# A state-space branch with chunks of eight tokens for four, unpadded matrices and lags through DRAM

## The chip, the cores and the metric

The kernel runs on one core of a Trainium2 chip. The metric is the device time of one execution in microseconds (us), the median of repeated runs.

## What is computed

One layer of a hybrid backbone over 512 latent tokens of 1024 channels with a context of 256 tokens. A conditioning vector gives shifts and scales for a first RMS norm; one input projection gives queries, keys, values, the state-space input u and two gates. A bidirectional diagonal state-space model of 32 groups with 64 complex states and 16 channels each runs over context and latent tokens, next to grouped attention; both are gated and merged, and a gated MLP with a width-3 convolution follows.

```python
def scan(bu_re, bu_im):                      # per direction, over tokens
    s_re, s_im = lax.associative_scan(_ssm_combine, (a_re, a_im, bu_re, bu_im), reverse=reverse, axis=1)
...
bu = einsum('blgp,gnp->blgn', u, bbar)       # complex, bbar from lambda, dt and b by zero-order hold
y += einsum('blgn,gpn->blgp', s_re, c_re) - einsum('blgn,gpn->blgp', s_im, c_im)
y += u * d
```

## The kernel before, in words

All matrices are fp32 split into a rounded part and a remainder: `weight` (line 126 on) loads a 256 KB piece on SP's queue into one of three `wr` buffers, ScalarE rounds it to `wh` (L128) and an engine named by the caller subtracts to `wl` (L129). `mm3` then issues three TensorE instructions per product, all recorded at L120.

The planner below the kernel orders the instructions of each engine by their order in the text and by a simulated readiness, so work of later lines fills gaps of earlier ones; each engine and SP's queue then run in that fixed order. The projection `proj` of the gates, 16 times, the keys, the values and two queries have no link to the branch and interleave with it. The attention phase reuses the memory of the branch's pool, and the GELU of the branch's result `y` precedes attention's exponentials on ScalarE, because the activation tables are changed in a fixed order (`table`, `act`).

Front: squares and their sums give the reciprocal root (`rstd_first`); x and ctx are multiplied by it on VectorE; then for each of eight row blocks the modulation row comes from TensorE (`mod_sums`, `mod_turn`), ScalarE applies scale and shift twice (once rounded, once not), VectorE subtracts, and TensorE accumulates u in `ul` and `uc`.

The branch cuts time into chunks of four tokens, so a scan has 192 steps. Channels are handled in four blocks `s` of 128, each of four pairs `k` of groups. `u` is written to DRAM and read back once, as 32 rows per token of a chunk. Lines before `s5_in` turn the parameters into powers of the step; most of that is on POOL (`DE`). `s5_in` and `s5_out` multiply b and c by the powers on POOL and place the results by half-height VectorE additions (L319) into zero-padded matrices `wpad` and `hpad`; the matrix of lags inside a chunk comes from TensorE (`kps`), is transposed on VectorE and copied by 32 partitions into `tp`. `turn` makes the sine and cosine tables of a pair, the additions on POOL.

`s5_pair`, 16 times: four transposes (`gps`), a copy (`gt`), four drive products of 192 columns into `gp` (a two-bank tile, tag "s", two buffers), rotation by the tables on VectorE (`p`), six scans, the rotation back (`ts`, on POOL but for a few), and five readout products of 128 columns into `yps`. `s5_end` copies 32 partitions at a time to `y`.

The helper `tt` (L319) records all element-wise products and sums of the branch, whichever the engine.

## Time and profile before

| | us |
|---|---|
| median of 3 runs | 1072.75 (1072.25 to 1072.86) |
| profiled execution | 1073.12 |
| its span | 1071.3 |

| engine | busy us | share of the span |
|---|---|---|
| TensorE | 947.3 | 88% |
| VectorE | 585.3 | 55% |
| ScalarE | 451.4 | 42% |
| POOL | 510.7 | 48% |

The shares are means over stages with different limits. The stages are: parameters, first norm and u up to about 88 us; the branch beside the projections up to about 350; attention up to about 675; then the output projection and the MLP. A product in fp32 is two TensorE instructions, one of a rounded operand is one.

### The profile page before, as it was taken

Reading aid. Unit: us, or ns where it says so; the run is one execution under the profiler, and the core shown is the slowest. Engines: PE = TensorE matmul, PEld = TensorE weight load, DVE = VectorE, ACT = ScalarE, POOL = GpSimd, SP = SyncE. Lnnn points to the kernel's source line nnn. Section 1 sums busy time; section 2 is a strip of 40 time slices with the busy share of each in tenths; the row PEclk is TensorE's granted clock in tenths of the full one; section 3 lists DMA queues with packets and bytes.
Section 4 is the critical chain, followed back from the end, with each engine's and each line's share of the span. In section 5 each row is a group of like instructions: output and inputs, shape, how many; then the busy total and the mean of one; then the engine's idle time right before and its main releaser. Section 6 shows DMA issues by size and latency. Waiting matters only on the chain.

```text
span 1071.3 us, 13697 instructions
## 1 busy us (share of the span) xinstructions
PE 947.3 (88%) x4978; PEld 770.2 (72%) x4978; DVE 585.3 (55%) x1069; ACT 451.4 (42%) x810; POOL 510.7 (48%) x496
## 2 busy tenths in 40 slices
PE   2978778898785898988989998999999999999996
PEld 1667677676674676756757688988888888888886
DVE  7544999979797766556655454543333323311103
ACT  6455345353532544343444234354444434433322
POOL 5865864536454335234220354055655556545553
PEclk9889989899898899998989999999999999999998
DMA  9515102121210131323223345023322332233332
GB/s 367 188 43 174 31 25 84 45 76 58 59 59 21 41 117 61 112 104 136 100 99 118 99 152 183 1 79 99 92 91 94 99 98 90 88 104 93 95 107 85
DMA packets 47604, 103.51 MB, mean 97 GB/s; under 512 B 5425, under 2 KB 11825, under 8 KB 43825
## 3 DMA queue, kind: packets, MB, share of 16 engines
q1 hardware_dynamic: 47536, 102.64, 29.1%
q8 instruction: 39, 0.64, 0.3%
q14 instruction: 29, 0.23, 0.1%
HBM read 98.95 MB, written 3.67 MB: 96 GB/s over the span
## 4 chain that ended last, share of the span: by engine, by line
PE 52%; DVE 13%; issue 8%; POOL 4%; ACT 3%; DMA 3%; DVEq 0%; POOLq 0%; ACTq 0%
PE up L120 23%; PE down L120 11%; PE proj L120 5%; PE po L120 3%; DVE p L319 2%; PE gb L120 2%; PE sc L120 2%; PE ga L120 2%; DMA wr<-wo 2%; DVE w L319 2%; POOL wl L129 1%; DVE nt L679 1%; DVE st L520 1%; ACT y L542 1%; DVE wl L129 1%
## 5 line engine op out<-in xcount | busy, mean ns | idle before, releaser
L129 POOL TENSOR_TENSOR wl<-wr,wh 128x512 fp32r<-128x512 f32 x194 | 253.3, 1324 | 369.3 <-ACT wh L128 362.1
L120 PE MATMUL up<-t,wh 128*128 128x512 f32 (+1 forms) x768 | 225.7, 378 | 1.6 <-DVE t L807 0.9
L128 ACT CAST wh<-wr 128x512 fp32r<-128x512 f32 x226 | 128.5, 609 | 110.6 <-PE down L120 36.1
L120 PEld LDWEIGHTS up<-t,wh 128*128 128x128 f32 x768 | 140.1, 188 | 32.1 <-DVE t L807 2.4
L120 PE MATMUL up<-t,wl 128*128 128x512 f32 (+1 forms) x384 | 144.8, 377 | 0.0
L120 PE MATMUL proj<-h,wh 128*128 128x512 f32 x384 | 129.7, 411 | 0.4 <-ACT wh L128 0.4
L120 PEld LDWEIGHTS proj<-h,wh 128*128 128x128 f32 x384 | 75.4, 197 | 19.0 <-DVE nb L718 1.5
L120 PE MATMUL proj<-h,wl 128*128 128x512 f32 x192 | 79.4, 413 | 4.9 <-DVE wl L129 4.9
L120 PEld LDWEIGHTS up<-t,wl 128*128 128x128 f32 x384 | 72.3, 188 | 14.6
L841 DVE SCALAR_TENSOR_TENSOR zc<-up,pv,zc 128x511 f32<-128x511 f32 x44 | 33.0, 751 | 88.4 <-ACT zc L840 88.4
L840 ACT ACTIVATE zc<-up,pv 128x512 f32<-128x512 f32 x44 | 34.1, 776 | 75.0 <-PE up L120 75.0
L319 DVE TENSOR_TENSOR w<-pw,pw 64x128 f32<-64x128 f32 x128 | 51.1, 431 | 22.9 <-POOL pw L319 20.6
L319 POOL TENSOR_TENSOR ts<-st,tab 128x512 f32<-128x512 f32 x28 | 39.4, 1424 | 34.0 <-DVE st L525 29.1
L872 DVE SCALAR_TENSOR_TENSOR x<-down,mods,x 128x512 f32<-128x512 f32 (+1 forms) x9 | 6.2, 691 | 87.8 <-PE down L120 87.8
L107 ACT ACTIVATE P<-sc,nb,rq 128x768 f32<-128x768 f32 x32 | 31.7, 993 | 52.3 <-DVE nb L718 32.5
L120 PEld LDWEIGHTS proj<-h,wl 128*128 128x128 f32 x192 | 38.1, 198 | 13.2 <-DVE wl L129 5.9
L717 DVE TENSOR_REDUCE nb<-sc 128x1 f32<-128x768 f32 x32 | 30.0, 952 | 31.0 <-PE sc L120 30.8
L120 PE MATMUL sc<-g,qh 128*128 128x512 f32 (+1 forms) x128 | 38.0, 363 | 7.4 <-ACT qh L128 5.5
L128 ACT CAST pth<-tps 128x512 fp32r<-128x512 f32 x48 | 27.9, 587 | 37.1 <-PE tps L730 31.2
L319 POOL TENSOR_TENSOR pw<-cb,hs 128x256 f32<-128x256 f32 x32 | 23.4, 747 | 38.4 <-DVE w L319 23.1
L120 PE MATMUL po<-ptl,g 128*128 128x512 f32 x48 | 23.6, 491 | 19.8 <-DVE ptl L129 19.7
L120 PE MATMUL yps<-ts,w 128*128 128x128 f32 x128 | 22.4, 312 | 20.1 <-DVE ts L319 11.5
(291 smaller groups left out, 2158.3 us busy)
## 6 DMA issues: line engine op xcount, KB each, us to landing
wr<-wup SPq DMA_DIRECT2D x88, 256.0 KB, 2.8
wmb<-wmB SPq DMA_DIRECT2D x16, 1024.0 KB, 5.8
wr<-wdn SPq DMA_DIRECT2D x40, 256.0 KB, 2.7
x<-x SPq DMA_DIRECT2D x4, 1024.0 KB, 6.5
g<-wmA SPq DMA_DIRECT2D x4, 1024.0 KB, 9.4
w<-wmA SPq DMA_DIRECT2D x4, 1024.0 KB, 11.2
wr<-wgs SPq DMA_DIRECT2D x16, 256.0 KB, 2.8
wr<-wga SPq DMA_DIRECT2D x16, 256.0 KB, 2.9
```

The lines of the kernel that those rows point to most:

```text
L107: i = A.activation(*a, **k).ins
L120: last[0] = T.matmul(ps, l, r, start=start, stop=stop).ins
L128: A.copy(hi, src)
L129: eng.tensor_tensor(lo, src, f(hi), op=OP.subtract)
L319: eng.tensor_tensor(o, a, b, op=op)
L520: V.tensor_tensor_scan(sv[0][:, ri, 0:192], rho[:, c0:c0 + 1].to_broadcast([128, 192]), p1[:, 0, ri], 0.0, op0=OP.mult, op1=OP.add)
L542: A.copy(y[32 * s:32 * s + 32, :, t::4], yps[32 * t:32 * t + 32].rearrange("p (k c) -> p k c", k=4))
L679: V.scalar_tensor_tensor(t, t, -0.5, xv, op0=OP.mult, op1=OP.mult)
L717: V.tensor_reduce(nb[:, b:b + 1], sv, axis=AX.X, op=OP.max)
L840: A.activation(z, ps, AF.Identity, scale=cw[1], bias=pv[:, PV_CB + i:PV_CB + i + 1])
L841: V.scalar_tensor_tensor(z[:, 1:512], ps[:, 0:511], cw[0], z[:, 1:512], op0=OP.mult, op1=OP.add)
L872: V.scalar_tensor_tensor(x1[i][:, c], ps[:, c], g2[:, i:i + 1], x1[i][:, c], op0=OP.mult, op1=OP.add)
```

## The change

Chunks have eight tokens, so a scan has 96 steps, and `u` has 16 rows per token. Two pairs of both directions go together: `s5_half` runs eight times, with eight scans of 96 columns each. Its operations are all on VectorE, those of `turn` too. `s5_build` makes the matrices `W` and `H` of a block without padding by six VectorE operations of 1024 elements each; a small `wpad` is filled by ScalarE. The lag matrix goes to DRAM and comes back shifted in eight pieces; `u` is read back per block, in eight pieces; the readout goes to DRAM and comes back as `y` in eight pieces. TensorE works in half arrays: drive products have 64 columns of weights, readout products 64 rows, and `y2` holds a two-bank tile of tag "s" for a whole block. The parameters' powers are computed on VectorE ahead of the first norm, for all exponents at once, with a change of activation tables there and back. The norm's multiply takes the modulation scale as well, which removes one ScalarE pass per row block. The gates' weight remainders go from VectorE to POOL. Host-side layouts of ctx, the parameters and `wglu` follow; the multiply after the GLU reads and writes tokens in the new order.

```diff
+TC = 8
+NC = (L + LC) // TC
+NL = L // TC
...
+    act(rho, ldt, AF.Exp, scale=float(TC))
...
+    def cmul(o, a, b, n):
+        c1, c2 = tz([8, 32], "bb", 2)[:, 0:n], tz([8, 32], "bb", 2)[:, 0:n]
+        br, bi = (b[:, None, i].to_broadcast([128, n, 32]) for i in range(2))
+        tt(c1, a[:, :, 0], br, OP.mult)
+        tt(c2, a[:, :, 1], bi, OP.mult)
+        tt(o[:, :, 0], c1, c2, OP.subtract)
+        tt(c1, a[:, :, 0], bi, OP.mult)
+        tt(c2, a[:, :, 1], br, OP.mult)
+        tt(o[:, :, 1], c1, c2, OP.add)
+    cmul(pw[:, 1:2], pw[:, 0:1], pw[:, 0], 1)
+    cmul(pw[:, 2:4], pw[:, 0:2], pw[:, 1], 2)
+    cmul(pw[:, 4:8], pw[:, 0:4], pw[:, 3], 4)
...
+    cmul(pf[:, 1:8], pw[:, 0:7], pf[:, 0], 7)
+    ws, hs = tz([2, 32, 8], "ws"), tz([2, 32, 8], "hs")
+    for o, i, up in ((ws, pf, 0), (hs, pw, 0)):
+        iv = i.rearrange("p e r (c d) -> p d r c e", d=2)
+        ov = o.rearrange("p r (c d) e -> p d r c e", d=2)
+        A.copy(ov[:, 0], iv[:, 0])
+        A.copy(ov[:, 1], iv[:, 1, :, :, ::-1])
...
-            V.tensor_tensor(src, src, rs, op=OP.mult)
-            A.activation(hi, src, AF.Identity, scale=am[:, k, m:m + 1], bias=shm[:, k, m:m + 1])
-            A.activation(src, src, AF.Identity, scale=am[:, k, m:m + 1], bias=shm[:, k, m:m + 1])
-            V.tensor_tensor(lo, src, f(hi), op=OP.subtract)
+            V.scalar_tensor_tensor(src, src, am[:, k, m:m + 1], rs, op0=OP.mult, op1=OP.mult)
+            A.activation(hi, src, AF.Identity, bias=shm[:, k, m:m + 1])
+            V.scalar_tensor_tensor(lo, src, shm[:, k, m:m + 1], f(hi), op0=OP.add, op1=OP.subtract)
...
+        us = k8("g12", [TC, NC + NL])
+        lat = ul[s // 2][:, s % 2].rearrange("p (c t) -> p t c", t=TC)[:, ::-1]
+        A.copy(us[:, :, NL:NC], uc[s // 2][:, 256 * (s % 2):256 * (s % 2) + 256].rearrange("p (t c) -> p t c", t=TC))
+        A.copy(us[:, :, 0:NL], lat)
+        V.tensor_copy(us[:, :, NC:NC + NL], lat)
+        ud = dram.tile([128, TC, NC + NL], F32, tag="ud", name="ud", bufs=4)
...
+    def s5_u(s):
+        u = tz([8, NC + NL], "u", 2)
+        for t in range(TC):
+            S.dma_start(u[16 * t:16 * t + 16], us_[s][:, t].rearrange("(j q) c -> q j c", j=8))
+        return u
...
+    def built(o, src, scal, s):
+        def by(a):
+            return scal[:, a, 8 * s:8 * s + 8, :, None].to_broadcast([128, 8, 8, 16])
+        b = [src[:, a, :, None, :].to_broadcast([128, 8, 8, 16]) for a in range(2)]
+        ov = [o[:, a].rearrange("p k (r q) -> p k r q", r=8) for a in range(2)]
+        for a in range(2):
+            t = tz([8, 8, 16], "t", 2)
+            tt(ov[a], b[0], by(a), OP.mult)
+            tt(t, b[1], by(1 - a), OP.mult)
+            tt(ov[a], ov[a], t, OP.add if a else OP.subtract)
+    def s5_build(s):
+        bb, cb_ = tz([2, 8, 16], "bb", 2), tz([2, 8, 16], "bb", 2)
+        S.dma_start(bb, io["sb"][s])
+        S.dma_start(cb_, io["sc"][s])
+        W, H = k8("k12", [2, 8, 128]), k8("w8", [2, 8, 128])
+        built(W, bb, ws, s)
...
+                src = ap_of(W[pa, ri, 0, 0:], [[256, 4], [128 + 112, 2], [1, 16]])
+                dst = ap_of(wpad[pa, ri, 0, g, 0:], [[64, 4], [32, 2], [1, 16]])
+                A.activation(dst, src, AF.Copy, scale=-1.0 if ri else 1.0)
+        built(H, cb_, hs, s)
...
+        for o, n, terms in ((0, 112, [(H[:, ri], 16, ri, 1) for ri in range(2)]),
+                            (112, 16, [(cb_[:, ri], 0, ri, d) for d in range(2) for ri in range(2)]),
+                            (128, 112, [(H[:, ri], 0, ri, 0) for ri in range(2)])):
+            for i, (m, c, ri, d) in enumerate(terms):
                 for k in range(4):
+                    T.matmul(kps[32 * k:32 * k + 32, o:o + n], wpad[:, ri, 2 * k + d].rearrange("p g q -> p (g q)"),
+                             m[:, 2 * k + d, c:c + n], start=i == 0, stop=i == len(terms) - 1, tile_position=(0, 32 * k))
+        lg = tz([240], "lg")
+        A.copy(lg, kps[:, 0:240])
+        V.scalar_tensor_tensor(lg[:, 112:128], cst[:, CS_D:CS_D + 16], sd[:, s:s + 1], lg[:, 112:128], op0=OP.mult, op1=OP.add)
+        ldr = dram.tile([128, 240], F32, tag="ldr", name="ldr", bufs=4)
+        S.dma_start(ldr, lg)
+        tp = tz([8, 128], "tp")
+        for r in range(TC):
+            S.dma_start(tp[16 * r:16 * r + 16], ldr[:, 16 * r:16 * r + 128].rearrange("(j q) l -> q j l", j=8))
+        blocks[s] = W, H, tp, s5_u(s)
...
+        wv, wq = tz([4, 6, 16], "t", 2), tz([4 * NC], "t", 2)
+        tt(wv, wa[:, c, :, None].to_broadcast([128, 4, 6, 16]), wb[:, c, None, :].to_broadcast([128, 4, 6, 16]), OP.add)
+        wv = wv.rearrange("p c a b -> p (c a b)")
         A.activation(wq, wv, AF.Identity, bias=magic)
         V.scalar_tensor_tensor(wv, wq, MAGIC, wv, op0=OP.subtract, op1=OP.subtract)
         A.activation(wq, wv, AF.Abs)
+        tab = tz([2, 4 * NC], "tab", 2)
+        act(tab[:, 0], wq, AF.Sin, scale=-TWO_PI_LO, bias=half_pi)
+        act(tab[:, 1], wv, AF.Sin, scale=-TWO_PI_LO)
+        tabs[n] = tab
...
+    def s5_drive(s, h):
+        W, H, tp, u = blocks[s]
+        gp = bank2("gp")
+        for k2 in range(2):
+            k = 2 * h + k2
+            gps = bank("gps", "b")
+            for d in range(2):
+                for ri in range(2):
+                    i = 2 * d + ri
+                    T.transpose(gps[:, 128 * i:128 * i + 128], W[:, ri, 2 * k + d], ident)
+            gt = tz([4, 128], "gt", 2)
+            A.copy(gt, gps.rearrange("p (i n) -> p i n", i=4))
+            for d in range(2):
+                c = slice(0, NC) if d else slice(NL, NL + NC)
+                o = NC * (2 * k2 + d)
+                for ri in range(2):
+                    for g in range(2):
+                        T.matmul(gp[64 * g:64 * g + 64, ri, o:o + NC], gt[:, 2 * d + ri, 64 * g:64 * g + 64],
+                                 u[:, 2 * k + g, c], start=True, stop=True, tile_position=(0, 64 * g))
+        return gp[:, :, 0:4 * NC]
+    def s5_half(s, h, gv, y2):
+        W, H, tp, u = blocks[s]
+        tab = tabs.pop(2 * s + h)
+        p1, p2, z = (tz([2, 4 * NC], "p", 3) for _ in range(3))
+        tt(p1, gv, tab[:, None, 0].to_broadcast([128, 2, 4 * NC]), OP.mult)
+        tt(p2, gv, tab[:, None, 1].to_broadcast([128, 2, 4 * NC]), OP.mult)
+        tt(p1[:, 0], p1[:, 0], p2[:, 1], OP.add)
+        tt(p1[:, 1], p2[:, 0], p1[:, 1], OP.subtract)
+        for i in range(4):
+            c = 8 * s + 4 * h + i
+            o = slice(NC * i, NC * i + NC)
             for ri in range(2):
+                zi, pi = z[:, ri, o], p1[:, ri, o]
+                if i % 2:
+                    zi, pi = zi[:, ::-1], pi[:, ::-1]
+                V.tensor_tensor_scan(zi, rho[:, c:c + 1].to_broadcast([128, NC]), pi, 0.0, op0=OP.mult, op1=OP.add)
+        q1, q2 = (t2().rearrange("p (r k c) -> p r k c", r=2, k=4) for _ in range(2))
+        zv = z.rearrange("p r (k d c) -> p d r k c", d=2, c=NC)
+        tv = tab.rearrange("p r (k d c) -> p d r k c", d=2, c=NC)
+        for j, q in enumerate((q1, q2)):
+            qv = q.rearrange("p r (k d) c -> p d r k c", d=2)
+            for d in range(2):
+                c = slice(1, 1 + NL) if d else slice(NC - NL - 1, NC - 1)
+                tt(qv[:, d], zv[:, d, :, :, c], tv[:, d, j, None, :, c].to_broadcast([128, 2, 2, NL]), OP.mult)
+        tt(q1[:, 0], q1[:, 0], q2[:, 1], OP.add)
+        tt(q1[:, 1], q1[:, 1], q2[:, 0], OP.subtract)
+        for k2 in range(2):
+            k = 2 * h + k2
+            o = slice(NL * k, NL * k + NL)
+            for g in range(2):
+                mm(y2[:, g, o], tp[:, 2 * k + g], u[:, 2 * k + g, NC:NC + NL], True, False)
+            for d in range(2):
+                for ri in range(2):
+                    for g in range(2):
+                        pa = slice(64 * g, 64 * g + 64)
+                        T.matmul(y2[:, g, o], H[pa, ri, 2 * k + d], q1[pa, ri, 2 * k2 + d], start=False,
+                                 stop=d + ri == 2, tile_position=(64 * g, 0))
+    def s5_end(s, y2):
+        ys = t2()
+        A.copy(ys.rearrange("p (k g c) -> p g k c", k=4, g=2), y2[:, :, 0:4 * NL].rearrange("p g (k c) -> p g k c", k=4))
+        yd = dram.tile([128, 8, NL], F32, tag="yd", name="yd", bufs=4)
+        S.dma_start(yd, ys.rearrange("p (j c) -> p j c", j=8))
+        for t in range(TC):
+            S.dma_start(y[:, s, NL * t:NL * t + NL], yd[16 * t:16 * t + 16].rearrange("p j c -> j p c"))
+    s5_build(0)
...
-        yps = bank("yps", "b")
-        for k in range(4):
-            s5_pair(4 * s + k, yps)
-            if 4 * s + k + 2 < 16:
-                turn(4 * s + k + 2)
-        s5_end(s, yps)
+        y2 = bank2("y2")
+        s5_half(s, 0, s5_drive(s, 0), y2)
+        gv = s5_drive(s, 1)
         if s < 3:
-            s5_in(s + 1)
-            s5_out(s + 1)
+            turn(2 * s + 2)
+            s5_build(s + 1)
+        s5_half(s, 1, gv, y2)
+        s5_end(s, y2)
+        if s < 3:
+            turn(2 * s + 3)
...
-        act(ms[i], proj(io["wgs"], i, "a", V), AF.Tanh, scale=0.5)
+        act(ms[i], proj(io["wgs"], i, "a"), AF.Tanh, scale=0.5)
...
-        gate_attn(i, V)
+        gate_attn(i, G)
```

## Rows read from the trace of the kernel before

**Rows 1.** Stages: us, busy (instructions) of PE, PEld, DVE, ACT, POOL; clock, DMA, GB/s
```profile
88.00:350.00 262.00, 206.74 (x1128) 173.78 (x1126) 228.71 (x416) 114.10 (x213) 149.43 (x143) 0.91 0.19 60
350.00:675.00 325.00, 294.81 (x1578) 230.47 (x1579) 194.88 (x357) 135.56 (x246) 105.39 (x79) 0.95 0.31 109
675.00:1071.00 396.00, 385.67 (x1867) 320.55 (x1865) 113.49 (x166) 152.63 (x263) 198.54 (x160) 0.99 0.29 89
```

**Rows 2.** Timeline, 318 to 333 us: start us, duration us, engine, line, operation
```profile
320.80 0.26 DVE L523 TENSOR_TENSOR_SCAN st<-sp,p 128x64 f32<-128x64 f32 x1
...
326.55 2.93 POOL L567 TENSOR_TENSOR tg<-tg,rsn 64x512 f32<-64x512 f32 x2
...
328.35 1.28 DVE L523 TENSOR_TENSOR_SCAN st<-sp,p 128x64 f32<-128x64 f32 x1
```

**Rows 3.** Groups, 88 to 350 us: busy us, mean ns, idle before and releasers
```profile
L319 DVE TENSOR_TENSOR w<-pw,pw 64x128 f32<-64x128 f32 x112 | 46.4, 446 | 18.9 <-POOL pw L319 18.4
...
L319 DVE TENSOR_TENSOR p<-p 128x384 f32<-128x384 f32 x32 | 31.7, 1030 | 0.3
L319 DVE TENSOR_TENSOR p<-gp,tab 128x768 f32<-128x768 f32 x32 | 29.1, 944 | 0.2
...
L129 DVE TENSOR_TENSOR wl<-wr,wh 128x512 fp32r<-128x512 f32 x32 | 27.1, 861 | 4.7 <-ACT wh L128 4.4
...
L525 DVE TENSOR_TENSOR_SCAN st<-sp,st,p 128x128 f32<-128x128 f32 x32 | 17.8, 582 | 0.1
...
L523 DVE TENSOR_TENSOR_SCAN st<-sp,p 128x64 f32<-128x64 f32 x32 | 15.5, 484 | 0.0
```

**Rows 4.** Timeline of DVE, 180 to 214 us, operations without POOL beside them
```profile
182.83 1.81 DVE L319 TENSOR_TENSOR p<-gp,tab 128x768 f32<-128x768 f32 x2
...
185.06 1.01 DVE L319 TENSOR_TENSOR p<-p 128x384 f32<-128x384 f32 x2
...
187.28 0.83 DVE L525 TENSOR_TENSOR_SCAN st<-sp,st,p 128x128 f32<-128x128 f32 x2
...
195.08 0.68 DVE L129 TENSOR_TENSOR wl<-wr,wh 128x512 fp32r<-128x512 f32 x1
...
210.95 0.96 DVE L319 TENSOR_TENSOR w<-pw,pw 64x128 f32<-64x128 f32 x4
```

**Rows 5.** Stage of line 319, then of line 129: us, busy of DVE, of POOL
```profile
88.00:350.00 262.00, 118.09 (x198) 108.66 (x111) 0.91 0.19 60
...
88.00:350.00 262.00, 33.17 (x42) 16.14 (x13) 0.91 0.19 60
```

**Rows 6.** Chain that ended last: start us, us, what
```profile
185.45 1.30 PE gp L120 x8
186.75 0.44 PE gps L498 x4
...
225.97 1.08 ACT y L542
...
343.27 0.91 PE yps L120 x8
...
412.83 5.50 PE proj L120 x24
```

**Rows 7.** Timeline of PE: two groups of lag products, eight instructions each
```profile
213.82 0.43 PE L450 MATMUL kps<-w,cp 128*32 128x128 f32 x8
214.06 0.40 PE L450 MATMUL kps<-w,pw 128*32 128x128 f32 x8
```

**Rows 8.** DMA issues of the page: KB each, median us to landing
```profile
ud<-p SPq DMA_DIRECT2D x4, 384.0 KB, 3.5
k<-ud SPq DMA_DIRECT2D x16, 96.0 KB, 3.0
```

**Rows 9.** Waits of SP's queue, 90 to 350 us: total, times, longest
```profile
SPq L140 <- DVE wl L129: 132.5, 32, 12.2
SPq L140 <- POOL wl L129: 59.0, 10, 19.1
```

More of the change, by code (lines that the diff above doesn't have):

```diff
@@ L30 @@
 WU_V = ()
-DISC_V = 0
 PO2 = 2
@@ new lines, in wrap @@
+    def wrap(a, r, n):
+        V.tensor_scalar(n, a, 1.0 / TWO_PI, MAGIC, op0=OP.mult, op1=OP.add)
+        V.tensor_scalar(n, n, MAGIC, None, op0=OP.subtract)
+        V.scalar_tensor_tensor(r, n, -C1, a, op0=OP.mult, op1=OP.add)
+        V.scalar_tensor_tensor(r, n, -C2, r, op0=OP.mult, op1=OP.add)
+        V.scalar_tensor_tensor(r, n, -C3, r, op0=OP.mult, op1=OP.add)
+    z1, z2, ang8 = sm("n"), sm("n2"), sm("a8")
+    r1, r8 = sm("r1"), sm("r8")
+    wrap(ang, r1, z1)
+    V.tensor_scalar(r1, r1, PI_LO, -PI_LO, op0=OP.min, op1=OP.max)
@@ new lines, in hybrid_layer_kernel @@
+    table("silu_and_others")
+    sn, co, ab = sm("sn"), sm("co"), sm("ab")
+    act(sn, r1, AF.Sin)
+    A.activation(ab, r1, AF.Abs)
+    act(co, ab, AF.Sin, scale=-1.0, bias=half_pi)
+    V.tensor_scalar(ang8, ang, float(TC), None, op0=OP.mult)
+    wrap(ang8, r8, z2)
+    fr, fhi, flo = sm("fr"), sm("fhi"), sm("flo")
+    V.tensor_scalar(fr, r8, 1.0 / TWO_PI, None, op0=OP.mult)
+    V.tensor_scalar(fhi, fr, 192.0, None, op0=OP.add)
+    V.tensor_scalar(fhi, fhi, 192.0, None, op0=OP.subtract)
@@ new lines, in hybrid_layer_kernel @@
+    cmul(pw[:, 1:2], pw[:, 0:1], pw[:, 0], 1)
+    cmul(pw[:, 2:4], pw[:, 0:2], pw[:, 1], 2)
+    cmul(pw[:, 4:8], pw[:, 0:4], pw[:, 3], 4)
+    den, nr, c1, c2 = sm("den"), sm("nr"), sm("c1"), sm("c2")
+    tt(c1, lr, lr, OP.mult)
+    tt(c2, li, li, OP.mult)
+    tt(den, c1, c2, OP.add)
+    V.reciprocal(den, den)
+    V.tensor_scalar(nr, pw[:, 0, 0], 1.0, None, op0=OP.subtract)
+    ni = pw[:, 0, 1]
+    tt(c1, nr, lr, OP.mult)
+    tt(c2, ni, li, OP.mult)
+    tt(c1, c1, c2, OP.add)
+    tt(pf[:, 0, 0], c1, den, OP.mult)
@@ new lines, in hybrid_layer_kernel, with by_s @@
+    kb = cst[:, CS_KB:CS_KB + 128].rearrange("p (c a) -> p c a", c=8)
+    wa, wb = tz([32, 6], "wa"), tz([32, 16], "wb")
+    for kk, w, n in ((ka, wa, 6), (kb, wb, 16)):
+        def by_s(t):
+            return t.rearrange("p (s c) a -> p s (c a)", s=4)
+        kx = kk.rearrange("p c a -> p (c a)")[:, None].to_broadcast([128, 4, 8 * n])
+        fh = fhi[:, :, None].to_broadcast([128, 32, n])
+        fl = flo[:, :, None].to_broadcast([128, 32, n])
+        ta, tq = tz([32, n], "p", 3), tz([32, n], "p", 3)
+        A.copy(by_s(ta), kx)
+        tt(tq, ta, fl, OP.mult)
+        tt(ta, ta, fh, OP.mult)
+        tt(w, ta, tq, OP.add)
+        V.tensor_scalar(tq, ta, MAGIC, None, op0=OP.add)
+        V.tensor_scalar(tq, tq, MAGIC, None, op0=OP.subtract)
+        tt(w, w, tq, OP.subtract)
@@ L296, in hybrid_layer_kernel @@
                 n == 0 and s % 2 == 0, n == KT - 1 and s % 2 == 1)
[L299 removed]
+    us_ = []
     dram = ctx.enter_context(tc.tile_pool(name="dram", bufs=1, space=bass.MemoryType.DRAM))
     for s in range(4):
[L302 to L308 removed]
@@ L449, in s5_in @@
                 for k in range(4):
-                    T.matmul(kps[32 * k:32 * k + 32, 128 * d:128 * d + 128], c[:, d * 4 + k], wpad[:, ri, d, k],
-                             start=ri == 0, stop=ri == 1, tile_position=(0, 32 * k))
-        lags = tz([8, 32], "pw2")
-        for o, i, n in ((0, 0, 3), (3, 4, 4), (7, 3, 1)):
-            V.transpose(lags[:, o:o + n].rearrange("p l q -> p (l q)"), kps[:, 32 * i:32 * i + 32 * n])
-        V.tensor_tensor(lags[:, 3], lags[:, 3], lags[:, 7], op=OP.add)
@@ L456, in s5_in @@
-        V.scalar_tensor_tensor(lags[:, 3], cst[:, CS_E:CS_E + 32], sd[:, s:s + 1], lags[:, 3], op0=OP.mult, op1=OP.add)
-        tp = tz([4, 4, 32], "tp")
-        for k in range(4):
-            for t in range(4):
-                z = lags[32 * k:32 * k + 32, t:t + 4][:, ::-1]
-                if (t + k) % 2:
-                    A.copy(tp[32 * t:32 * t + 32, k], z)
-                else:
-                    V.tensor_copy(tp[32 * t:32 * t + 32, k], z)
-        blocks[s] = cb_, tp
-    def s5_out(s):
-        cols = slice(8 * s, 8 * s + 8)
-        for e in range(1, 5):
-            padded(blocks[s][0], hs[:, e], cols, hpad, (e - 1, 4 - e))
@@ L540, in s5_end @@
-    def s5_end(s, yps):
-        for t in range(4):
-            A.copy(y[32 * s:32 * s + 32, :, t::4], yps[32 * t:32 * t + 32].rearrange("p (k c) -> p k c", k=4))
-    s5_in(0)
+        tab = tz([2, 4 * NC], "tab", 2)
[22 more added lines that the diff above has]
+        return gp[:, :, 0:4 * NC]
```

249 lines of the change are left out of this document (48 added, 201 removed).

## The prediction

> **What bounds the kernel now.** I read the span by stages first [rows 1]. From 675 us on TensorE is busy 385.7 of 396 us, and the change touches nothing there. Attention, 350 to 675, has it busy 294.8 of 325 us (91%). The stage before, 88 to 350 us, is the poor one: 206.7 of 262 us. That is where the state-space branch runs, with the gate, key, value and first query projections as filler on TensorE. The reader should see in that row that VectorE is busy 228.7 us, 87%.
>
> But that busy time is inflated. A scan of 64 columns takes 0.26 us when POOL is idle and 1.28 us when it falls on a POOL instruction [rows 2]: both work on SBUF operands and one stands while the other runs. The means show the same against undisturbed ones: 64x128 placements 446 ns against 0.96/4 = 240; 384-element sums 1030 against 1.01/2 = 505; scans of 128 columns 582 against 415; of 64, 484 against 260; weight remainders 861 against 680 [rows 2 to 4]. With the counts that is 112 x 0.206 + 32 x (0.525 + 0.167 + 0.224 + 0.181) = 58 us of pure waiting in VectorE's 228.7. The 768-element products read PSUM and stand at 944 ns whether POOL runs or not (undisturbed 1.81/2 = 905); they don't take part. So some 170 us of VectorE work, 142 of it (without 32 x 0.9) exclusive with POOL, meets POOL's 149.4 us [rows 1]: 291 in a window of 262, POOL's figure holding waits too. **The stage is full of VectorE plus POOL**, not of TensorE. Of POOL's 149.4 us, 108.7 are the branch's own element-wise work [rows 5].
>
> **The change part by part.** Undisturbed VectorE time goes at about 0.09 us plus 1.15 ns per element (from 128 in 240 ns and 512 in 680) [rows 4].
>
> *Matrices.* Removed: the 128 half-height placements on VectorE and the POOL multiplies ahead of them, the 32-partition copies of lags, and POOL's whole 108.7 us. Added on VectorE: two builds of six 1024-element operations per block of channels: 12 x 1.27 = 15.2 us, four blocks 61 us. The first needs nothing of u and is taken to run ahead of 88 us; 46 stay in the stage (61 if it doesn't, and then the pair below is level with TensorE).
>
> *Half blocks, eight for sixteen pairs.* Products from PSUM 2 x 0.9; two 384-element sums 1.0; eight scans of 96 columns, between 0.26 and 0.415: 8 x 0.3 = 2.4; six operations of 256 elements, 6 x 0.39 = 2.3. Sum 7.5 us, eight times 60 us, of which 14.4 read PSUM. Turn tables, six left in the stage: (0.5 + 0.5) x 6 = 6. Lag and key/value remainders: 7.
> VectorE in the stage: 46 + 60 + 6 + 7 = 119 us, 105 of it exclusive with POOL.
>
> *Gates.* 32 remainders move from VectorE to POOL at 16.14/13 = 1.24 us [rows 5]: 40 us. POOL then has 149.4 - 108.7 + 40 = 81 us. VectorE plus POOL: 105 + 81 = **186 us, for 291 now**.
>
> *TensorE.* Now: 128 drive instructions at 1.30/8 = 162 ns, 160 readout ones at 0.91/8 = 114, 64 transposes at 110, 128 lag ones at (214.06 - 213.82)/8 = 30 [rows 6, 7]: 21 + 18 + 7 + 4 = 50 us; the other 157 us of the 206.7 are projections with their waits. A block of 24 projection instructions takes 5.50 us, and 18 of them are 99 us; value and key add (144 + 32) x 0.115 + 48 x 0.229 = 31, sums of squares some 7: 137 us of pure pace, an estimate. After: 256 drive instructions of half the columns into half the array: 81 ns if they don't overlap, 40 if two column tiles run side by side as the four of the lags do: 10 to 21. Readout: 64 full and 256 half-height instructions of 64 columns. 114 ns is what one with 128 columns takes, so 320 x 0.114 = 36 us if the half-height ones cost as much, 22 if two row halves overlap. Lags 256 x 0.03 = 8, transposes 7. Sum 47 to 72, taken 60, since the lags row, the only tiled one here, shows overlap for columns but no row shows it for row halves. TensorE in the stage: 184 to 209, taken 197.
> The Trainium skill (TensorE: Matmul & The Clock Gate, LDWEIGHTS) says that a weight load costs by its columns and not by its rows, so that half-height matrices save nothing. By it alone the readout stands at its high end. The same page (Packing small matmuls) lets loads overlap where the row groups differ, as they do here between neighbours. No row of before decides it.
>
> *What is late next.* TensorE at 197, the exclusive pair at 186: the bound passes to TensorE, as in attention, where it manages 91% beside a chain of softmax and remainders. 197/0.91 = 216 us for 262: **-46 us**. Bounds: 184/0.97 = 190 (-72) and 209/0.85 = 246 (-16).
>
> *DRAM trips.* Per block the lag matrix goes out and comes back in 8 pieces, u in 8, y in 8: 4 x 27 issues on SP's queue. A store lands in 3.5 us, a piece in 3.0 [rows 8]. Inside the stage they lie beside filler. At its end the last y has nothing behind it except gates left over: 3.5 + 3.0 and 8 issues, 4 us at most = 10.5 us where four copies of 1.08 stood [rows 6], +6 if uncovered, 0 if covered. Attention's exponentials stand behind the GELU of y on ScalarE, so they would wait too. Taken: +3.
>
> *Front.* The discretisation puts about 60 small operations of some 0.22 us (a 128-element one takes 0.24 [rows 4]) on VectorE ahead of the first norm, 13 us, and takes the same off POOL. The 16 multiplies by the reciprocal root, 8 x (0.68 + 0.35) = 8 us, no longer stand ahead of the first modulated row; they are done after it, one by one, in place of one of the two ScalarE passes. So +13 - 8 = +5 where nothing covers it, and 0 where the small operations, which need only the parameters, run while x is still being loaded. Counted 0; bounds +5 and -6, a gain since the projection's weight remainders no longer queue behind the matrices on POOL (five of them at 1.24).
>
> Sum against the profiled execution of 1073.1 us: -46 + 3 + 0 = 1030; the median lies 0.4 lower, which changes nothing. **1030 us.**
>
> **The rivals.**
> *1. The chain through the halves stays serial.* The readout accumulator is a two-bank tile held for a whole block, so of two such slots the drive has one; the next block's drive may have to wait for readout (40 x 0.114 = 4.6), its copy 1.1 and that of the transposes 1.1 at most, transposes 0.9, drive 2.6: 10.3 us of empty VectorE, three times 31. Then VectorE's 119 + 81 of waiting for POOL at worst + 31 + 10.5 = 241 us from the first drive, some 9 us after 88 (a store, pieces and issues): the stage ends at 338, not at 350, and the kernel at 1061. For: only one slot turns over. Against: turns, remainders and the next build fill such gaps.
>
> *2. SP's queue, slower than before.* SP issues in order, and its weight loads wait for a free buffer: 132.5 + 59.0 us in 42 waits here, up to 19.1 [rows 9]. Now they delay filler only, because u is fetched once at the start. Afterwards u, the lags and y of every block stand in that queue, each pair with a store to wait for. One round behind a mean wait of 4.6 is 15 us, lags and y in series 30 per block; four blocks are 121 us of chain. If half is uncovered, +61 eats the 46 and the time is 1089. The point from which it decides: 46/4 = 11.5 us of uncovered trip per block. For: u, lags and y are each needed by the next step. Against: the waits come from remainders being late on a crowded VectorE, the very thing that goes; and a next block's lags are only wanted after 8 us of its half.
> The Trainium skill (DMA: Bandwidth & Descriptors, Rules for kernel authors) says that transfers under 64 KB are mostly overhead and should be joined; y's 32 KB pieces break it. The 96 KB piece's 3.0 us is the nearest row; the rule would leave y's the same.
>
> *3. It doesn't do what it says.* The folded multiply must now wait for the modulation row, and the discretisation delays the first norm: with +5 at the front, the stage at 246 and +6 at its end the time is 1068; with one more uncovered trip it lands on 1073.
>
> **How the numbers follow.** Forecast 0.70, at 1030 with its own bounds 1001 to 1057; rival 1 0.17; rival 2 0.10; rival 3 0.03. The range holds forecast and rival 1: 1001 to 1063. Faster by over 0.2% (some 2 us, about what a measurement here can tell from no change): 0.87; within: 0.03; slower: 0.10.
>
> **What would show it.** Right: attention's first scores some 45 us earlier than 350; POOL's line-319 group gone; VectorE's means near the undisturbed ones; TensorE above 88% in the stage. Rival 1: VectorE idle before the products of each block's first half, released by the drive. Rival 2: TensorE or VectorE idle behind a DMA of u, tp or y, SP waiting for remainders just ahead. The forecast is wrong if the half-height readout costs over 114 ns apiece, or if the stage is as long with a less busy VectorE.

## The result, and the profile after

The changed kernel takes 1031.8 us (median of 4 runs, 1024.0 to 1032.4) against 1072.6 for the kernel before beside it: ratio 0.960 [0.956, 0.965]. The prediction was 1030. The profiled execution took 1032.4 us, its span is 1030.4.

Where the 40.9 us of span went is best read from the starts of a few TensorE groups:

| start of, us | before | after | stretch that ends there: before, after |
|---|---|---|---|
| first drive product `gp` | 100.5 | 97.3 | front: -3.2 |
| last readout product | 343.9 | 261.0 | branch: 243.4, 163.7 (-79.7) |
| first attention scores | 350.5 | 312.3 | left-over filler: 6.6, 51.3 (+44.7) |
| first MLP product | 673.4 | 632.9 | attention: 322.9, 320.6 (-2.3) |
| end of the span | 1071.3 | 1030.4 | rest: 397.9, 397.5 (-0.4) |

The branch itself became 80 us shorter, and 45 of them went straight back: the gates' projections, which used to be done by the time the branch ended, are now done behind it. From the first drive to the first scores 35 us are gained.

Stages of after, as in [rows 1]: us, busy (instructions) of PE, PEld, DVE, ACT, POOL; granted clock, DMA share, GB/s.

```profile
88.00:312.00 224.00, 203.74 (x1520) 171.22 (x1520) 143.18 (x223) 85.53 (x158) 101.76 (x62) 0.94 0.31 93
312.00:633.00 321.00, 291.93 (x1541) 228.10 (x1541) 193.89 (x350) 128.92 (x241) 107.10 (x79) 0.94 0.31 109
633.00:1030.00 397.00, 387.30 (x1879) 322.07 (x1878) 113.94 (x170) 152.57 (x265) 199.37 (x160) 0.99 0.28 89
```

TensorE is busy 203.7 of 224 us, 91%, where it was 79% [rows 1]. VectorE lost 86 us of the stage's work, POOL 48.

Groups of VectorE and POOL in 88 to 312 us of after, as in [rows 3]: busy us, mean ns of one, idle before and what ended it.

```profile
L131 POOL TENSOR_TENSOR wl<-wr,wh 128x512 fp32r<-128x512 f32 x43 | 76.4, 1794 | 109.6 <-ACT wh L130 106.5 <-DMA wr<-wga 2.8
...
L530 DVE TENSOR_TENSOR_SCAN p<-sp,p 128x96 f32<-128x96 f32 x64 | 28.5, 512 | 0.0
...
L225 DVE TENSOR_TENSOR p<-gp,tab 128x768 f32<-128x768 f32 x16 | 14.7, 949 | 23.1 <-PE gp L509 23.1
...
L225 DVE TENSOR_TENSOR p<-p 128x384 f32<-128x384 f32 x16 | 12.0, 788 | 0.1
...
L225 DVE TENSOR_TENSOR tg<-tg 128x256 f32<-128x256 f32 x16 | 10.6, 702 | 0.1
...
L225 DVE TENSOR_TENSOR k<-k,t 128x1024 f32<-128x1024 f32 x6 | 7.2, 1208 | 0.0
```

POOL's group of line 319 is gone [rows 5]; its place is taken by 43 weight remainders at 1794 ns on average, where one took 1240 before [rows 5]. VectorE still waits for POOL: 788 ns for a 384-element sum (505 undisturbed, [rows 4]), 702 for a 256-element one that takes 415 in the kernel a_gates_dve below. The 768-element products, which read PSUM, stand at 949, as before. The Trainium skill (GPSIMD Engine Reference, Specifications) says that POOL shares its SBUF interfaces with VectorE and collides with VectorE instructions that have two SBUF inputs; both lines agree, since only the product has a single one.

Four pieces of after's chain of waits: start us, us, what.

```profile
128.51 1.04 PE y L550 x16
129.55 0.59 PE y L122 x4
...
193.01 1.50 PE gp L509 x32
...
261.26 25.98 PE proj L122 x114
```

A half-height readout instruction costs 1.04/16 = 65 ns, not 114, one of full height with as many columns (a lag product, second line) 0.59/4 = 148, a half-width drive 1.50/32 = 47. The last line is the filler that is left when the branch is done.

Waits in 88 to 312 us of after: engine, line, what it waited for, us in total, times, longest.

```profile
DVE w L131 <- ACT w L130: 38.4, 1, 38.4
...
DVE p L225 <- PE gp L509: 23.1, 5, 10.5
...
PE kps L464 <- DVE w L225: 8.7, 4, 4.9
```

The first is VectorE standing idle behind the branch until the GELU of y is taken, the second is its waits for the drive inside the branch. The third is the longest of TensorE's waits: its lag products (`kps`) wait for the matrix that VectorE builds. For POOL's remainders TensorE waits only 2.8 us there.

The end of the branch in after: ScalarE copies the last readout, SP sends it out and fetches y, and ScalarE takes the GELU of y only behind the last gate (start us, us; ScalarE first, then SP).

```profile
261.30 0.59 ACT L555 COPY tg<-y 128x512 f32<-128x512 f32 x1 [6.26 <-PE y L550]
...
290.86 1.92 ACT L109 ACTIVATE y<-y 128x2048 f32<-128x2048 f32 x1
```
```profile
261.92 0.33 SPq L557 DMA_DIRECT2D yd<-tg  x1
263.98 4.95 SPq L559 DMA_DIRECT2D y<-yd  x8
```

The trip is over by about 272 us and is wanted at 291.

### The profile page after: what moved, and what is told of

It is laid out like the page before. It is cut to its first block, busy times and chain, and to the rows that moved or that the text cites. A ratio compares the mean times of both kernels' runs of the same rounds, so it can differ in the third digit from the quotient of the medians.

```text
span 1030.4 us, 14205 instructions
## 1 busy us (share of the span) xinstructions
PE 946.4 (92%) x5394; PEld 769.6 (75%) x5394; DVE 518.1 (50%) x902; ACT 409.6 (40%) x746; POOL 431.3 (42%) x326
## 4 chain that ended last, share of the span: by engine, by line
PE 70%; DVE 19%; DMA 4%; issue 2%; ACT 2%; POOL 1%; SPq 0%; DVEq 0%; POOLq 0%; ACTq 0%
PE up L122 24%; PE down L122 12%; PE proj L122 8%; PE po L122 5%; PE sc L122 3%; DVE p L530 2%; DVE p L225 2%; DMA wr<-wo 2%; DVE t L225 2%; PE pab L122 2%; PE ga L122 2%; DVE k L225 2%; PE gb L122 2%; PE tps L749 2%; PE mods L363 2%
## 5 line engine op out<-in xcount | busy, mean ns | idle before, releaser
L131 POOL TENSOR_TENSOR wl<-wr,wh 128x512 fp32r<-128x512 f32 x226 | 320.7, 1438 | 527.0 <-ACT wh L130 516.7
L122 PE MATMUL proj<-h,wh 128*128 128x512 f32 x384 | 123.8, 398 | 0.4 <-ACT wh L130 0.4
L122 PEld LDWEIGHTS proj<-h,wh 128*128 128x128 f32 x384 | 73.0, 191 | 18.3 <-DVE nb L737 1.5
L122 PE MATMUL proj<-h,wl 128*128 128x512 f32 x192 | 75.9, 395 | 0.9 <-POOL wl L131 0.9
L131 DVE TENSOR_TENSOR ptl<-tps,pth 128x512 fp32r<-128x512 f32 x48 | 32.5, 685 | 12.6 <-ACT pth L130 12.6
L122 PE MATMUL po<-pth,g 128*128 128x512 f32 x96 | 36.7, 468 | 0.3 <-ACT pth L130 0.3
L122 PE MATMUL down<-h,wh 128*128 128x512 f32 x112 | 35.6, 389 | 0.0
L122 PEld LDWEIGHTS sc<-g,qh 128*128 128x128 f32 x128 | 24.7, 197 | 13.2 <-ACT P L109 5.6
## 6 DMA issues: line engine op xcount, KB each, us to landing
wmb<-wmB SPq DMA_DIRECT2D x16, 1024.0 KB
x<-x SPq DMA_DIRECT2D x4, 1024.0 KB
g<-wmA SPq DMA_DIRECT2D x4, 1024.0 KB
w<-wmA SPq DMA_DIRECT2D x4, 1024.0 KB
```

What stands on the lines that cost most here:

```text
L122: last[0] = T.matmul(ps, l, r, start=start, stop=stop).ins
L131: eng.tensor_tensor(lo, src, f(hi), op=OP.subtract)
```

## The experiments

Differences are of medians, against 1031.8 for the changed kernel; the kernel before gave 1072.6 to 1074.4 beside the various groups, so 2 us are within the drift. The planner deals out a new order for every edit: attention takes 314 to 323 us in the profiles of the changed kernel and of the variants that leave it alone. So differences of a few us are not read.

### Does POOL's work stop VectorE? (before)

**b_gates_pool**: one part of the change alone, the gates' remainders on POOL.

```diff
-        act(ms[i], proj(io["wgs"], i, "a", V), AF.Tanh, scale=0.5)
+        act(ms[i], proj(io["wgs"], i, "a"), AF.Tanh, scale=0.5)
-        gate_attn(i, V)
+        gate_attn(i, G)
```

> The kernel before (1072.6 us) with one part of the change: the gates' 32 weight remainders go from VectorE to POOL. Theory (VectorE and POOL exclude each other on SBUF operands, so their sum sets the stage): VectorE loses 32 x 0.68 = 22 us, POOL gains 32 x 1.24 = 40, the sum rises by 18: the same or slower, 1073 to 1091. Rival (VectorE's own busy time sets the stage, POOL is a free helper): 27 us of VectorE's busy time go, 1046 to 1060.

1078.6 us, ratio 1.004 [1.002, 1.006]. Stage of b_gates_pool, columns as above:

```profile
88.00:350.00 262.00, 212.32 (x1115) 178.14 (x1115) 229.29 (x377) 113.86 (x212) 182.49 (x169) 0.88 0.19 58
```

VectorE has 39 instructions fewer than in [rows 1], 32 of them the remainders, and is busy as long, 229.3 against 228.7: what it was relieved of came back as waiting for POOL.

**b_branch_dve**: the opposite, all element-wise work of the branch on VectorE.

```diff
-        eng.tensor_tensor(o, a, b, op=op)
+        V.tensor_tensor(o, a, b, op=op)
```

> The kernel before with the branch's element-wise products and sums all on VectorE, none on POOL; nothing else changed. Theory: POOL's 108.7 us become 28 x 0.68 + 56 x 0.39 + 13 x 0.57 + 14 x 0.39 = 54 us on VectorE and the 58 us of waiting go with them; the pair falls from some 283 to 196 + 41 = 237 us: not slower, 1045 to 1073. Rival (POOL relieves VectorE): VectorE's 228.7 us grow by 54 to 283, the stage by 21 to 54: 1094 to 1127.

1059.3 us, ratio 0.987 [0.984, 0.990], against 1094 to 1127 if the two worked side by side.

```profile
88.00:336.00 248.00, 196.32 (x1095) 166.97 (x1095) 228.68 (x518) 110.19 (x199) 42.11 (x32) 0.89 0.18 57
```

VectorE does 102 instructions more than in [rows 1] in the same 228.7 us of busy time: what it took over was paid by waits that went, so the two engines do exclude each other. The gain itself lies mostly ahead of the stage. The edit also takes the products and sums of the discretisation off POOL, and the first drive comes at 88.9 us for 100.5; from there to the first scores (335.8) it is 246.9 us for 250.0. So the run refutes the rival, but that the sum of the two engines set the length of the stage it does not show: VectorE alone is still busy 92% of it. The Trainium skill (Perfetto Trace Analysis, Optimizing Scalar/DVE Operations) warns that shifting work between these two engines might not help. Here shifting it back to VectorE made the kernel 15 us faster, 12 of them at the front.

### What bounds the changed kernel?

**a_two_products**: the gates' products with the weight remainder are left out, 16 x 8 instructions of 0.229 us, 29 us of TensorE; the remainders are still computed.

```diff
+            if low:
+                mm3(ps, (w[0][:, k], w[1][:, k]), (hh[k], hl[k]), k == 0, k == KT - 1)
+            else:
+                mm(ps, w[0][:, k], hh[k], k == 0, False)
+                mm(ps, w[0][:, k], hl[k], False, k == KT - 1)
```

> The changed kernel (1031.8 us) with the gates' product of the weights' remainder left out (two TensorE instructions per step for three; its output is less exact); loads, roundings and remainders stay. Theory (TensorE is the bound after the change): 16 x 8 x 0.229 = 29 us of TensorE go, of which 85 to 100% show: 1002 to 1007. Rival (the chain of halves through VectorE ends the stage): 1030 to 1032.

1012.6 us, ratio 0.944 [0.940, 0.948]: 19 of the 29 us, between the two ranges on record. TensorE matters, but not alone. In the profiled execution, the longest of the four (1018.2), the first scores come only 8.5 us earlier (303.8). Stage of a_two_products, columns as above:

```profile
88.00:296.00 208.00, 175.38 (x1366) 146.66 (x1366) 147.25 (x221) 84.47 (x156) 89.87 (x58) 0.89 0.33 97
```

TensorE is busy 84% of it, with a granted clock of 0.89 for 0.94: it waits more, not less, once it has less to do. Two of its waits in 88 to 310 us of a_two_products, for the matrix of the lags and for the readout's input, both from VectorE:

```profile
PE kps L464 <- DVE w L225: 9.1, 3, 8.0
PE y L550 <- DVE tg L225: 8.8, 3, 4.3
```

**a_build_twice**: the matrix `H` of each block is built a second time, 4 x 6 x 1.2 = 29 us of VectorE on SBUF operands, 22 of them in the stage (the first block is built ahead of it).

```diff
         built(H, cb_, hs, s)
+        built(H, cb_, hs, s)
```

> The changed kernel with the six operations that build H done twice for each block: 4 x 6 x 1.27 = 30 us more of VectorE, 23 of them inside the stage. Theory (TensorE is the bound, the branch ends 26 us ahead of the last gate): 1031 to 1040. Rival (the chain through VectorE is the bound): 1055 to 1063.

1059.7 us, ratio 0.986 [0.983, 0.990]. The theory of 1031 to 1040 fell: VectorE's work does not lie hidden under TensorE's. POOL's row in the trace of a_build_twice (start us, us) and the longest wait of TensorE in 88 to 310 us there show how the added time reaches the kernel:

```profile
248.80 17.41 POOL L131 TENSOR_TENSOR wl<-wr,wh 128x512 fp32r<-128x512 f32 x3 [6.30 <-ACT wh L130]
```
```profile
PE proj L122 <- POOL wl L131: 14.5, 2, 12.5
```

Three remainders took 17.4 us, one of them 14.9 by itself, and TensorE waited 12.5 us in one piece for a remainder. These waits, 14.5 us in all, are half of what the edit cost; the other half is not broken down here.

**a_psum_products**: the same 29 us of VectorE, but in products that read PSUM, each done three times.

```diff
+        for _ in range(2):
+            tt(p1, gv, tab[:, None, 0].to_broadcast([128, 2, 4 * NC]), OP.mult)
+            tt(p2, gv, tab[:, None, 1].to_broadcast([128, 2, 4 * NC]), OP.mult)
```

> The changed kernel with the two products that read the drive from PSUM done three times over: 4 x 0.9 us in each of eight halves, 29 us more of VectorE, as much as the doubled build added, but on operations that didn't stand still beside POOL. If the doubled build cost 28 us because VectorE's chain got longer: 1055 to 1063 again. If it cost them because the build shuts POOL's remainders out of SBUF: 1032 to 1042.

1033.2 us, ratio 0.960 [0.956, 0.963]. The products are there,

```profile
L225 DVE TENSOR_TENSOR p<-gp,tab 128x768 f32<-128x768 f32 x48 | 43.2, 946 | 26.3 <-PE gp L509 26.3
```

and the last readout comes 30 us later (290.7 for 261.0), but the median is only 1.4 us higher. The four runs lie between 1028.7 and 1041.9. The profiled one is the longest of them: its first scores come 7.5 us later (319.8), and there the GELU of y starts at 300.3 for 290.9, after a wait of 4.0 us for y itself. So a branch that is 30 us longer is about as much as the left-over filler covers. VectorE's time as such and the length of the branch's chain cost little up to there; what costs is VectorE's time on SBUF operands. One difference stays untested: the doubled build also makes VectorE's unbroken run longer (no gap from 244.4 to 262.6 us in a_build_twice), the doubled products come a few at a time.

**a_no_remainders**: a_two_products, and the gates' remainders are not computed either, about 40 us less on POOL.

```diff
+            if low:
+                split(r, pieces[1], pieces[2], eng)
+            else:
+                A.copy(pieces[1], r)
```

> The kernel with two products per gate step (1012.6 us), and the gates' weight remainders, which it no longer reads, not computed either: POOL loses 32 x 1.24 = 40 us, TensorE nothing. If POOL beside VectorE still costs the changed kernel time: 985 to 1005. If only TensorE and VectorE's own work count: 1009 to 1015.

991.9 us, ratio 0.923 [0.921, 0.925]: another 20.7 us, taken from an engine that is busy 43% of the stage in a_two_products. TensorE reads these remainders in neither kernel, so it is not their lateness that cost the time. What went are TensorE's waits for VectorE. The same two in 88 to 310 us of a_no_remainders:

```profile
PE kps L467 <- DVE w L228: 1.5, 3, 0.7
...
PE y L553 <- DVE tg L228: 0.2, 1, 0.2
```

The granted clock of the stage is 0.95 for 0.89. The loads' `wr` buffers no longer wait for POOL to read them either; what part that has in the 20.7 us these runs do not separate.

**a_gates_dve**: the changed kernel with the gates' remainders back on VectorE.

```diff
-        act(ms[i], proj(io["wgs"], i, "a"), AF.Tanh, scale=0.5)
+        act(ms[i], proj(io["wgs"], i, "a", V), AF.Tanh, scale=0.5)
-        gate_attn(i, G)
+        gate_attn(i, V)
```

> The changed kernel (1031.8 us) with the gates' 32 remainders back on VectorE. Rival (this move is where the gain came from): 20 to 27 us come back, 1052 to 1059. Theory (VectorE and POOL exclude each other): VectorE does 32 x 0.68 = 22 us more, POOL 40 less, and half of VectorE's some 35 us of waiting for POOL goes: 1025 to 1040.

**1015.7 us**, ratio 0.945 [0.943, 0.948]: 16 us better than the changed kernel and the best complete kernel of this study. Both the expectation and its rival were too slow.

```profile
88.00:303.00 215.00, 200.10 (x1528) 167.03 (x1527) 150.34 (x259) 85.17 (x159) 40.45 (x31) 0.96 0.34 99
```

VectorE's busy time rises by 7 us only for 32 more remainders of 0.68 us, 22 in all: the other 15 were paid by waits that went. A 256-element sum, 702 ns in after, is down to 415, and TensorE's wait for the matrix `w` ahead of the lag products shrinks from 8.7 us to 3.5 (a_gates_dve, 88 to 310 us: a group, a wait).

```profile
L225 DVE TENSOR_TENSOR tg<-tg 128x256 f32<-128x256 f32 x16 | 6.0, 415 | 0.0
```
```profile
PE kps L464 <- DVE w L225: 3.5, 1, 3.5
```

From the first drive (99.4) to the first scores (302.8) it is 203.4 us, 11.6 less than in the changed kernel. Of the parts of the change that were undone one by one here, the move of these remainders to POOL is the only one that costs time.

**a_all_dve**: the key, value and query weights' remainders on VectorE as well.

```diff
-        w = weight(io["wk"][g], [KT, 128])
+        w = weight(io["wk"][g], [KT, 128], V)
-    wv_ = [weight(io["wv"][i], [4, 256]) for i in range(2)]
+    wv_ = [weight(io["wv"][i], [4, 256], V) for i in range(2)]
-        ps = proj(io["wq"], h, "b")
+        ps = proj(io["wq"], h, "b", V)
```

> The changed kernel with the gates' weight remainders on VectorE, as in a_gates_dve (1015.7 us), and those of key, value and query weights as well, so that POOL has hardly any work left between 88 and 310 us. Theory: POOL's 37.7 us that are left there still stop VectorE, each operation on either side standing while the other runs. Moved onto VectorE, where a remainder is 0.68 us undisturbed against 1.24 on POOL, they cost about half: 1006 to 1013. Rival: with the gates' remainders gone TensorE, busy 197 of 212 us, bounds the stage, and more work on VectorE only lengthens its queue: 1016 to 1022.

1036.9 us, ratio 0.965 [0.961, 0.969]: 21 worse than a_gates_dve, outside both ranges. Waits of TensorE in 88 to 310 us of a_all_dve, then SP's queue in its timeline:

```profile
PE vp L122 <- DVE wl L131: 7.0, 1, 7.0
PE y L122 <- DMA tp<-ldr: 4.9, 2, 3.3
...
PE y L122 <- DMA yd<-tg: 3.3, 1, 3.3
```
```profile
170.10 15.84 SPq L142 DMA_DIRECT2D wr<-wgs  x5
...
197.04 4.94 SPq L559 DMA_DIRECT2D y<-yd  x8
```

The first is a wait for a remainder in VectorE's own queue. The other two, 8.2 us, are the mechanism of rival 2: the weight loads stand in SP's queue until VectorE has taken its turn at a remainder, and lags and y stand behind them. TensorE's waits in that window grow from 15 us in a_gates_dve to 26; that is half of the 21, and what the other half is stays open.

**a_gates_dve_fill**: a_gates_dve with four attention gates moved as filler into attention's heads 4 to 7.

```diff
-NGA = 8
-FILL = [[("glu", 2 * i), ("glu", 2 * i + 1)] for i in range(4)] + [[]] * 4
+NGA = 4
+FILL = [[("glu", 2 * i), ("glu", 2 * i + 1)] for i in range(4)] + [[("gate", 4 + i)] for i in range(4)]
```

> The changed kernel with the gates' remainders on VectorE (a_gates_dve, 1015.7 us), and four of the eight attention gates' projections placed as filler of attention heads 4 to 7 in place of the branch's stage. A gate is 5.5 us of TensorE, so 22 us leave the stage. Theory: TensorE bounds the stage there by now (197 of 212 us busy), and attention's stage has some 29 us of idle TensorE that takes part of the 22: 1004 to 1011. Rival: attention's gaps are links of its own chain, a gate there displaces a head's work, and the time stays or grows: 1015 to 1026.

1024.2 us, ratio 0.953 [0.950, 0.957], in the rival's range. The first scores come 27 us earlier (275.4 for 302.8), the first MLP product 4 later: attention's idle TensorE time is not free for a gate.

### The parts that were counted at nothing

**a_trips_twice**: lag matrix and y make the trip to DRAM twice, through a hop in SBUF.

```diff
+        S.dma_start(lg2, ldr)
+        ldr = dram.tile([128, 240], F32, tag="ldr2", name="ldr2", bufs=4)
+        S.dma_start(ldr, lg2)
...
+        S.dma_start(ys2, yd)
+        yd = dram.tile([128, 8, NL], F32, tag="yd2", name="yd2", bufs=4)
+        S.dma_start(yd, ys2)
```

> The changed kernel, with the lag matrix and the result of each block sent through DRAM twice: each goes out, comes back to SBUF, goes out again and comes back as before. Each extra hop is a store and a load, 3.5 and 3.0 us by the trace of before, so 6.5 us for each of eight trips. Theory: a trip inside the stage lies under the other block's element-wise work and TensorE's filler, and the last one, of y, ends under the gates left over, some 25 us ahead of the GELU that wants it. Then the time stays within 7 us of the changed kernel's 1031.8: 1031 to 1038. Rival: the trips are on the chain of the stage. Half of eight extra hops uncovered gives +26, all of them +52: 1058 to 1084.

1030.7 us, ratio 0.959 [0.956, 0.962]. An extra hop on each of eight trips, 6.5 us apiece by the estimate in the expectation, is covered, and so is the trip itself. Rival 2 did not come about.

**a_unfolded**: the first norm's four operations as before.

```diff
-            V.scalar_tensor_tensor(src, src, am[:, k, m:m + 1], rs, op0=OP.mult, op1=OP.mult)
-            A.activation(hi, src, AF.Identity, bias=shm[:, k, m:m + 1])
-            V.scalar_tensor_tensor(lo, src, shm[:, k, m:m + 1], f(hi), op0=OP.add, op1=OP.subtract)
+            V.tensor_tensor(src, src, rs, op=OP.mult)
+            A.activation(hi, src, AF.Identity, scale=am[:, k, m:m + 1], bias=shm[:, k, m:m + 1])
+            A.activation(src, src, AF.Identity, scale=am[:, k, m:m + 1], bias=shm[:, k, m:m + 1])
+            V.tensor_tensor(lo, src, f(hi), op=OP.subtract)
```

> The changed kernel with the first norm as before: multiply by the reciprocal root, two ScalarE passes with scale and shift, a subtraction. Theory (the front counted about 0): 1031 to 1036. Rival (the fold brings the front's 6 us): 1037 to 1042.

1041.3 us, ratio 0.971 [0.966, 0.975], the rival's range: 9.5 us. But the first drive is only 1.6 us later (98.9). The rest is lost in the stage. Here is one place of it, in the timelines of POOL, VectorE and TensorE of a_unfolded:

```profile
219.56 10.90 POOL L131 TENSOR_TENSOR wl<-wr,wh 128x512 fp32r<-128x512 f32 x3 [6.30 <-ACT wh L130]
```
```profile
219.48 2.33 DVE L225 TENSOR_TENSOR t<-bb,hs 128x1024 f32<-128x1024 f32 x2
221.73 1.42 DVE L225 TENSOR_TENSOR tg<-p,tab 128x256 f32<-128x256 f32 x4
223.08 2.35 DVE L225 TENSOR_TENSOR w<-w,t 128x1024 f32<-128x1024 f32 x2
225.35 0.74 DVE L225 TENSOR_TENSOR tg<-tg 128x256 f32<-128x256 f32 x2
226.02 0.54 DVE L225 TENSOR_TENSOR t<-wa,wb 128x384 f32<-128x384 f32 x1
227.30 0.80 DVE L484 SCALAR_TENSOR_TENSOR t<-t 128x384 f32<-128x384 f32 x1 [0.74 <-ACT t L483]
```
```profile
227.73 0.79 PE L122 MATMUL proj<-h,wl 128*128 128x512 f32 x1 [6.66 <-POOL wl L131]
```

VectorE runs without a gap from 219.5 to 226.6. A remainder that POOL began at 219.6 is done only at 227.7, when the gap comes, and TensorE has stood 6.7 us for it.

**a_disc_late**: the discretisation moved back behind the projection of u, its lines unchanged but for the last: the change back of the activation tables is left out.

```diff
-    zt = tz([20, 32], "zt")
...
     def sum_squares(acc, src, i, last, ps):
...
     def s5_u(s):
...
+    zt = tz([20, 32], "zt")
...
```

> The changed kernel, with the discretisation moved back behind the input projection, where it stood before; all else as changed. Theory: in the changed place its 13 us of small VectorE operations run while x is being loaded and cost nothing; behind the projection they stand ahead of the first build and drive, where nothing of the branch can run, so the time grows by 0 to 13 us over 1031.8: 1032 to 1045. Rival: in the changed place they delay the first norm, and behind the projection the filler covers them: 1020 to 1031.

1048.9 us, ratio 0.976 [0.973, 0.978]: 17 us, above the theory's 13. u is complete 10 us sooner (last `ul` product at 68.4 for 78.1), the first drive 3 us sooner, and the stage is then longer by more than that: TensorE is busy 140 of the 174 us from 88 to 262 (156 in the changed kernel), with waits like these (88 to 310 us):

```profile
PE kps L462 <- DVE w L327: 10.7, 4, 3.8
PE y L122 <- DMA tp<-ldr: 10.4, 2, 7.5
PE proj L122 <- POOL wl L131: 7.7, 2, 6.2
```

The activation tables matter here too: ScalarE takes the norm of the first keys behind the sine tables of two turns, at 105.8 us, where the changed kernel takes it at 90.9. How much of the 9.5 and the 17 us belongs to the edits themselves, and how much to the tables and to where the planner's new order lets a remainder or a trip fall, these runs do not separate.

## Why the prediction was right, point by point

**The bound before: the exclusion is right and shown, the sum is not.** VectorE and POOL exclude each other on SBUF operands; b_gates_pool and b_branch_dve went as that says and against the rival, and a_psum_products shows that PSUM readers stand outside. That VectorE plus POOL set the length of the stage is not shown: in b_branch_dve the pair was to fall by 46 us (283 to 237 in its expectation), and the stretch from first drive to first scores became 3 us shorter.

**The sum: right by parts that miss in both directions.** Stage: -46 predicted, -35 from first drive to first scores. Trips: +3 predicted, 0. Front: 0 predicted, -3.2. Attention and after: 0 predicted, -2.7. That a gain put 11 us too high in the stage and gains put 9 too low elsewhere nearly cancel is luck.

**TensorE in the stage: two terms mis-sized.** The branch's own products: drive 256 x 0.047 = 12, readout 256 x 0.065 = 17, with the lag products of full height, 64 x 0.59/4 = 9, lags 8 and transposes 7 as put: 53 us, where 60 was taken. The row halves do overlap, which no row of before could tell. The Trainium skill (TensorE: Matmul & The Clock Gate, Packing small matmuls) lets weight loads overlap with running products where the row groups differ, and 65 ns beside 148 for full height agrees. The weight loads themselves, of half and of full height, in 88 to 312 us of after (busy us together, mean ns of one):

```profile
L550 PEld LDWEIGHTS y<-tg,w 64*128 64x128 f32 x256 | 19.0, 221 | 4.5 <-DVE tg L225 2.1 <-issue 1.0 <-DVE t L225 0.4
...
L122 PEld LDWEIGHTS y<-u,tp 128*128 128x128 f32 x64 | 9.2, 206 | 1.7 <-issue 0.4
```

One load of half height lasts no less than a full one, but 256 of 221 ns are 57 us and fit into 19.0, so they run beside one another.

The other products take 203.7 - 53 = 151 us, where 137 was called pure pace: stretches at the lower clock are in it (last section), also those of the branch's own products. At the 91% that was taken, and came, 203.7 for 197 makes the stage 224 us for 216.

**"TensorE at 197, the exclusive pair at 186: the bound passes to TensorE" is the step that failed.** TensorE is indeed busy 91%, as taken. But the smaller sum is not hidden by the larger. What was put in or taken out, and what came of it in the kernel (medians) and in the stage (profiled execution, first drive to first scores):

| edit | us on the engine | us of the kernel | us of the stage |
|---|---|---|---|
| TensorE, a_two_products | -29 | -19 | -9 |
| POOL, a_no_remainders after a_two_products | -40 | -21 | -25 |
| VectorE on SBUF, a_build_twice | +29, 22 in the stage | +28 | +27 |
| VectorE on PSUM, a_psum_products | +29 | +1 | +5 |

A microsecond of POOL's work, of TensorE's and of VectorE's on SBUF operands is worth 0.5, 0.7 and 1.0 in the kernel; in the stage TensorE's, which was to be the bound, weighs least of the three. They take turns at being last. The links are two, and both are inputs of TensorE. Where VectorE runs back to back, POOL's remainder does not get through and TensorE's filler waits for it (a_build_twice, a_unfolded). Where POOL works, VectorE stands, and the lag products and the readout wait for what VectorE makes; this is the link that a_no_remainders and a_gates_dve relieve, and in the changed kernel itself it is the larger one (8.7 us for `w`, 2.8 for remainders). The prediction added VectorE's and POOL's times and compared the sum with TensorE's; it left out that both deliver what TensorE works on. Nor did VectorE's means come near the undisturbed ones, which it had named as a sign of being right: 788 ns for 505. The 40 us that the change put on POOL are the main piece: without them the stage is 11.6 us shorter (a_gates_dve), as much as the 11 us by which it fell short.

**Trips and rival 2**: right that they are covered; +3 was not needed. The mechanism is real, as a_all_dve shows with 8.2 us (and a_disc_late with 10.4 us of waits for the lags), but it does not appear in the changed kernel's order.

**Rival 1**: its bubble is there, VectorE waits 23.1 us for the drive where it waited 0.2 [rows 3], near the 31 put on it. The reason given for it is not seen: no drive product waits for a slot; the drive at 193 us stands in TensorE's order behind readout, transposes and 20 instructions of filler. The bubble cost little: a_psum_products, which delays the branch by 30 us more, has a median 1.4 us higher, because the stage ends on the left-over filler and not on the branch.

**Front**: the 13 us were right. In the trace of after some 69 operations, of 32 to 512 elements, take 13.2 us of VectorE from start to start, between 3 and 22 us and among the sums of squares. They are covered but for little: u's first product starts at 26.5 us, and at 25.2 in a_disc_late, where part of them comes later. That both moves would cost 10 to 17 us if undone was not foreseen; see the open point above.

**What no run takes apart.** The gates' remainders, the fold and the place of the discretisation were undone one by one. The chunks of eight tokens, the unpadded matrices and the half arrays were not, so their own share of the 41 us is not measured.

## What to carry to other kernels

When two engines exclude each other, add their times, but then ask whose input the excluded one produces: a sum that lies 6% below the next bound is not hidden if it delivers what that bound works on. A cheap operation on the weaker of the two is best given back to the stronger until its queue holds up the loads, and both sides of that point can be measured with one argument changed (1031.8, 1015.7, 1036.9). A shorter chain is worth only what the work beside it leaves: here 80 us shorter were worth 35.
